# Stick-breaking's v, q and k turned in 32 by 32 blocks on VectorE instead of whole on TensorE

## The chip, the cores and the metric

The kernel runs on one core of one Trainium2 chip. The metric is the device time of one execution in microseconds (us); for a kernel it is the median of its runs. TensorE is the matrix engine, VectorE, ScalarE and GpSimd (POOL in the profile) work on tiles in SBUF and PSUM, and SyncE (SP) issues most of the DMAs. Every engine, and every DMA queue of an engine, works through its instructions in the order in which the program holds them.

## The reference

One layer of a hybrid decoder, batch 1, 1,024 tokens and 16 learned meta tokens in front of them (1,040 positions), width 1,024, all in float32: a half-step SwiGLU, a mixer, another half-step SwiGLU. The mixer projects the normed rows once and splits the columns into an HGRN2 part (4 heads of 128) and a stick-breaking part (8 heads of 64). The change touches stick-breaking alone:

```
q = rms_norm(split_heads(q_raw, 8), q_gain)
k = rms_norm(split_heads(k_raw, 8), k_gain)
v = split_heads(v_raw, 8)
z = q @ k.T / sqrt(64)                      # per head, 128 queries at a time
log_beta = where(allowed, log_sigmoid(z), -inf)
log_keep = where(allowed, log_sigmoid(-z), 0)
suffix = cumsum(log_keep, from the right) - log_keep
out = exp(log_beta + suffix) @ v
```

A key is allowed when it lies strictly before the query. The norm is over the 64 numbers of one head at one position.

## The kernel before

Weights and activations are held as pairs of a rounded part and a remainder (`wh`, `wl` and `xh`, `xl`), and a product is three matmuls: `xh` with `wh`, `xh` with `wl`, `xl` with `wh` (`product`, L242 to L253).

`run` works in stages: the first SwiGLU, the norm, the mixer's projections, the attention woven with the HGRN2 projections, HGRN2, the output projection, the second SwiGLU. The change lies in the projections of stick-breaking. Two heads make one pair, and there are four pairs. `sb_project` (L1260) projects for a pair the 128 columns of k, of v and of q; the columns lie along the partitions and the tokens along the free axis. For pair 0 most of this is done ahead, so only the second half of q is left. The chunks of k and v are 512, 264 and 264 tokens (`CHUNKS`), those of q twice 512 (`HALVES`); a chunk is 24 matmuls. ScalarE copies each chunk from PSUM into `kT`, `vTs` or `qT`.

The weights of a column come by `col_tile` (L237) and `split_w` (L213): SP loads 512 KB into `raw` (two buffers, L225), ScalarE casts `wh` (L232), VectorE makes `wl` (L234); `wh` and `wl` have three buffers each, so a cast waits until the projection three columns earlier is done with its buffer.

The attention wants v with the tokens along the partitions. `sb_v` (L1305) therefore turns `vTs` on TensorE, up to four 128 by 128 tiles in one PSUM bank (`flip`, L1363), splits it into a rounded part and a remainder (ScalarE, VectorE) and stores both with one DMA for each group of four tiles into `vD`. `sb_qk` (L1324) turns q and k in the same way, squares (ScalarE), sums over each head's 64 columns (VectorE), copies the turned tiles to `nat` (VectorE), takes root and reciprocal, multiplies on POOL, turns each tile back on TensorE (`back`, L1355), multiplies by the gain (ScalarE) and splits and stores the result with `put_split` (L1295: ScalarE casts, POOL subtracts, SP stores) into `qD` and `kD`.

`sb_jobs` (L1369) loads q, k and v of one head at a time from these and yields the attention's steps. It begins with stores of zeros into the rows of `vD` that belong to no meta token (L1452).

The order of work: within the stage TensorE's instructions stand as they are written out, in the order in which `weave` (L1585) draws them. It takes a step of the projections, adds the step's cost to a clock, and takes a step of `sb_v` or `sb_qk` whenever that generator's due time has come; each `yield` of these names the cost on TensorE and the delay until the next step. The instructions of the other engines and of SP are put in order by a scheduler with a time model of its own. A pair's generators must have ended before the projections of the second pair after it begin (`join`). After the four pairs the 16 first steps of the HGRN2 projections run (v and f of its head 0), then `braid` mixes attention and the remaining projections.

x at the kernel's beginning is already turned in the manner that the change uses (L983 to L989): VectorE transposes 32 by 32 blocks, and four stores put the blocks in place, in pieces of 128 bytes.

Of the kernel before, what the change touches and what calls it, by code (L numbers as in the profile page):

```python
# [20 lines left out]
P = 128  # L21
D = 1024
KT = D // P
SEQ = 1024
META = 16
T = META + SEQ
# [14 lines left out]
class Block:  # L41
# [1218 lines left out]
    def sb_project(self, p, xh, xl, pool, mix, dst):  # L1260
        nc = self.nc
        vT = pool.tile([P, T], F32, tag="vTs", name="vTs", bufs=2)
        kT = pool.tile([P, T], F32, tag="kT", name="kT", bufs=2)
        qT = pool.tile([P, SEQ], F32, tag="qT", name="qT", bufs=2)
        def use_q(ps, ci, c0, n):
            s = slice(c0 - META, c0 - META + n)
            nc.scalar.copy(qT[:, s], ps)

        def use_k(ps, ci, c0, n):
            nc.scalar.copy(kT[:, c0 : c0 + n], ps)  # L1270

        def use_v(ps, ci, c0, n):
            nc.scalar.copy(vT[:, c0 : c0 + n], ps)

        w = None
        if p == 0:
            w = self.early_w
            for use, x, ci in ((use_k, "k", 0), (use_v, "v", 1), (use_v, "v", 2), (use_v, "v", 0),
                               (use_k, "k", 1), (use_k, "k", 2)):
                use(self.early[x][ci], ci, *CHUNKS[ci])  # L1280
            use_q(self.early["q"][0], 0, *CHUNKS[0])
            self.after_early()
        else:
            yield from self.project(xh, xl, 2560 + P * p, CHUNKS, use_k)
            yield from self.project(xh, xl, 3072 + P * p, CHUNKS, use_v)
        done = [self.sb_v(p, vT, mix, dst[2]), self.sb_qk(p, qT, kT, pool, mix, dst)]
        rest = self.project(xh, xl, 2048 + P * p, HALVES[: 1 if p == 0 else 2], use_q, w)
        if p == 0:
            yield next(rest)
        yield "start", done[0]  # L1290
        yield from rest
        yield "start", done[1]
        return done

    def put_split(self, dst, k, s, t, pool):  # L1295
        nc = self.nc
        n = t.shape[1]
        hi = pool.tile([P, n], F32R, tag="ohi", name="ohi", bufs=2)
        lo = pool.tile([P, n], F32R, tag="olo", name="olo", bufs=2)
        nc.scalar.copy(hi, t)  # L1300
        nc.gpsimd.tensor_sub(lo, t, hi.bitcast(F32))
        nc.sync.dma_start(dst[k, :, 0, s], hi.bitcast(F32))
        nc.sync.dma_start(dst[k, :, 1, s], lo.bitcast(F32))

    def sb_v(self, p, vT, mix, vD):  # L1305

        nc = self.nc
        for j0, nj, m in self.groups:
            ps = self.flip(vT, [self.spots[j0 + j] for j in range(nj)])
            ps = ps.rearrange("p j (h d) -> p j h d", h=2)  # L1310
            t = mix.tile([P, 4, 2, 2, 64], F32R, tag="vhl", name="vhl", bufs=2)
            hi, lo = (t[:m, :nj, :, i, :] for i in range(2))
            nc.scalar.copy(hi, ps[:m])
            nc.vector.tensor_sub(lo, ps[:m], hi.bitcast(F32))
            nc.sync.dma_start(
                vD[p, :m, j0 : j0 + nj, :],
                t.bitcast(F32)[:m, :nj].rearrange("p j h i d -> p j (h i d)"),
            )
            yield 430, 1500

    groups = [(1, 4, P), (5, 4, P), (0, 1, META)]
    spots = [(0, META)] + [(META + P * j, P) for j in range(8)]

    def sb_qk(self, p, qT, kT, pool, mix, dst):  # L1324
        nc = self.nc
        groups, spots = self.groups, self.spots
        ss = pool.tile([P, 17, 2], F32, tag="sbs", name="sbs", bufs=2)
        nc.vector.memset(ss, 1.0)
        nat = pool.tile([P, 17, P], F32, tag="nat", name="nat", bufs=2)
        rows = [(qT, 8 + j0, nj, m, [((j0 - 1 + j) * P, P) for j in range(nj)])  # L1330
                for j0, nj, m in groups[:2]]
        rows += [(kT, j0, nj, m, [spots[j0 + j] for j in range(nj)]) for j0, nj, m in groups]

        for src, j0, nj, m, at in rows:
            ps = self.flip(src, at)
            sq = pool.tile([P, 4, P], F32, tag="sq4", name="sq4", bufs=2)
            nc.scalar.activation(sq[:m, :nj], ps[:m], AF.Square)
            nc.vector.tensor_reduce(
                ss[:m, j0 : j0 + nj, :].rearrange("p j h -> p (j h)"),
                sq[:m, :nj].rearrange("p j (h d) -> p (j h) d", h=2),  # L1340
                mybir.AxisListType.X, ALU.add,
            )
            nc.vector.tensor_copy(nat[:m, j0 : j0 + nj, :], ps[:m])
            yield 430, 600
        nc.scalar.activation(ss, ss, AF.Sqrt, bias=self.eps, scale=1.0 / 64)
        nc.vector.reciprocal(ss, ss)
        for _, j0, nj, m, _ in rows:
            t = nat[:m, j0 : j0 + nj, :].rearrange("p j (h d) -> p j h d", h=2)
            r = ss[:m, j0 : j0 + nj, :].unsqueeze(3).broadcast_to([m, nj, 2, 64])
            nc.gpsimd.tensor_mul(t, t, r)  # L1350
        yield 0, 6000
        for src, j0, nj, m, at in rows:
            ps = self.ptr.tile([P, 4, P], F32, tag="tr", name="back")
            for j in range(nj):
                nc.tensor.transpose(ps[:, j, :m], nat[:m, j0 + j, :], self.ident[:m, :m])  # L1355
            s0, n = at[0][0], (nj - 1) * P + m
            t = mix.tile([P, 512], F32, tag="gt", name="gained", bufs=2)[:, :n]
            gain, to = (self.qg8, dst[0]) if src is qT else (self.kg, dst[1])
            nc.scalar.mul(t, ps.rearrange("p j t -> p (j t)")[:, :n], gain[:, 0:1])
            self.put_split(to, p, slice(s0, s0 + n), t, mix)  # L1360
            yield 430, 1500

    def flip(self, src, spans):  # L1363
        ps = self.ptr.tile([P, len(spans), P], F32, tag="tr", name="flip")
# [4 lines left out]
    def sb_jobs(self, keys, fetch, pool):  # L1369


        nc = self.nc
        qD, kD, vD, oD = keys
# [4 lines left out]
        def load(p, hh):  # L1378
            rows = slice(64 * hh, 64 * hh + 64)
            qs = fetch.tile([P, SEQ], F32R, tag="qs", name="qs", bufs=2)  # L1380
            ks = [fetch.tile([P, T], F32R, tag=f"ks{i}", name="ks", bufs=2) for i in range(2)]
            for i in range(2):
                part = slice(64 * i, 64 * i + 64)
                nc.sync.dma_start(qs.bitcast(F32)[part], qD[p, rows, i])
                for j in range(2):
                    nc.sync.dma_start(ks[j].bitcast(F32)[part], kD[p, rows, j])
            return qs, ks

        def load_v(p, hh):
            v = fetch.tile([P, 9, P], F32R, tag="v", name="v", bufs=2)  # L1390
            nc.sync.dma_start(v.bitcast(F32), vD[p, :, :, hh * P : (hh + 1) * P])
            return v

        def job(p, hh, qs, ks, v, b0):
# [55 lines left out]
            nc.vector.memset(t.bitcast(F32), 0.0)  # L1450
        none = kept["wm"][1][1].rearrange("p b t -> p (b t)").bitcast(F32)[META:]
        for p in range(4):  # L1452
            nc.sync.dma_start(vD[p, META:, 0], none)
        ahead, v = load(*heads[0]), load_v(0, 0)
        yield None
        pool = pools[0]
        for i, (p, hh) in enumerate(heads):
            qs, ks = ahead
            if i:
                v = load_v(p, hh)  # L1460
            for b0 in (0, 6, 2, 4):
# [172 lines left out]
    def run(self):  # L1634
        nc, tc, a = self.nc, self.tc, self.a
# [4 lines left out]
        vD = self.dram.tile([4, P, 9, 2 * P], F32, name="vD")  # L1640
# [6 lines left out]
        n = 512  # L1647
# [8 lines left out]
        with ExitStack() as c0:  # L1656
            with ExitStack() as c1:
# [121 lines left out]
                with tc.manual_schedule(engines={nc.tensor.engine}), ExitStack() as c2:  # L1779
# [46 lines left out]
                    v = [nc.vector] * 2  # L1826
# [202 lines left out]
                with tc.manual_schedule(engines={nc.tensor.engine}):  # L2029
# [20 lines left out]
                    for i, n in enumerate(LEVELS[:5]):  # L2050
                        m = self.masks[:, i, :].rearrange("p (b h r) -> p b h r", h=2, r=n)
# [30 lines left out]
            with tc.manual_schedule(engines={nc.tensor.engine}), ExitStack() as cx:  # L2082
                with ExitStack() as c1:
                    mix = self.pool("mix2", ctx=c1)
# [99 lines left out]
                r = self.inv_rms_rows(sums[1], n, px, ppb)  # L2184
# [55 lines left out]
```

## Time and profile before

| | |
|---|---|
| median of 3 runs | 2021.64 us (2020.22 to 2021.96) |
| the profiled execution | 2020.56 us, its span 2018.8 us |
| granted TensorE clock of that execution | 0.999 |
| stage from the second half of pair 0's q to the first attention step | 748.72 to 899.74 us |
| matmuls that turn q, k, v in it (`flip` and `back`) | 172 |

The profile is one execution of the program. PE is TensorE's matmul, PEld its weight load, DVE VectorE, ACT ScalarE; SPq is SP's DMA queue. Times of instructions count from the span's start. A timeline row has start, duration, engine, line, operation, output and inputs, shapes and count, and behind them, in brackets, the idle time before it and what ended that. Matmuls overlap: their starts are recorded, their ends are modelled, so the distance of two starts is what one costs. A group's row has its count, its busy time in us, the mean of one in ns, and the engine's idle time just before with what ended it.

### The profile page before, as it was taken

How to read it: one execution, taken by the hardware profiler on the slowest of the kernel's cores; microseconds unless marked ns; L12 is line 12 of the kernel's file. 1: busy time of each engine (PE TensorE's matmuls, PEld its weight loads, DVE VectorE, ACT ScalarE, POOL GpSimd, SP SyncE). 2: the span in 40 equal slices, each digit the busy share in tenths (PEclk: the TensorE clock that was granted, in tenths of full speed). 3: DMA queues.
4: the chain of work that ended last, by engine and by line, in shares of the span. 5: the costliest groups of instructions: out<-in, count | busy, mean ns of one | idle time of the engine just before them, and what ended most of it. 6: DMA issues, size and time to landing. Idle time of an engine off the chain costs nothing.

```text
span 2018.8 us, 30806 instructions
## 1 busy us (share of the span) xinstructions
PE 1964.1 (97%) x10940; PEld 1646.2 (82%) x10940; DVE 1356.4 (67%) x2052; ACT 860.8 (43%) x1742; POOL 583.5 (29%) x692
## 2 busy tenths in 40 slices
PE   7999999999999999999999999999999999999998
PEld 6788777777878888888888888777888888888887
DVE  7867667787578663237767667558566766767764
ACT  6423333333444544456666635434132333344443
POOL 3443233332000002334333341320444545530000
PEclk9999999999999999999999999999999999999999
DMA  6266787757985416343545166664533233369363
GB/s 206 83 171 182 227 260 245 241 185 255 327 278 164 131 53 204 123 169 101 139 133 139 55 229 179 167 238 162 194 102 110 101 103 103 106 253 310 116 198 136
DMA packets 315578, 347.19 MB, mean 172 GB/s; under 512 B 61520, under 2 KB 216656, under 8 KB 315424
## 3 DMA queue, kind: packets, MB, share of 16 engines
q1 hardware_dynamic: 297136, 292.18, 46.0%
q0 software_dynamic: 17248, 53.03, 7.5%
q8 instruction: 87, 1.43, 0.3%
q14 instruction: 67, 0.55, 0.1%
q10 hardware_dynamic: 1040, 0.00, 0.0%
HBM read 233.75 MB, written 111.38 MB: 171 GB/s over the span
## 4 chain that ended last, share of the span: by engine, by line
PE 82%; DVE 7%; DMA 5%; issue 3%; ACT 2%; POOL 1%; SPq 0%; DVEq 0%; POOLq 0%; ACTq 0%
PE o L685 18%; PE qb L430 16%; PE qc L430 11%; PE qa L430 10%; PE proj L249 5%; PE proj L251 5%; PE proj L250 5%; PE flip L1366 2%; DMA raw<-in_ffn_w_out_dram 1%; PE wo L250 1%; PE wo L249 1%; PE wo L251 1%; PE mq L937 1%; PE oacc L1436 1%; PE oacc L1438 1%
## 5 line engine op out<-in xcount | busy, mean ns | idle before, releaser
L430 PE MATMUL qb<-T,wh 128*128 128x512 f32 x1056 | 346.0, 391 | 10.1 <-DVE u L462 7.5
L430 PEld LDWEIGHTS qb<-T,wh 128*128 128x128 f32 x1056 | 198.1, 188 | 58.4 <-ACT both L174 5.7
L430 PE MATMUL qa<-B,wh 128*128 128x512 f32 x696 | 227.0, 390 | 2.2 <-DVE sum L513 1.9
L362 DVE TENSOR_TENSOR wl<-s,wh 128x512 fp32r<-128x512 f32 x160 | 183.4, 1147 | 60.4 <-ACT wh L360 59.3
L249 PE MATMUL proj<-xh,wh 128*128 128x512 f32 (+2 forms) x640 | 216.5, 338 | 0.8 <-DVE st L1059 0.7
L685 PE MATMUL o<-t,w 128*128 128x512 f32 x924 | 213.1, 391 | 1.3 <-DVE w L618 1.1
L251 PE MATMUL proj<-xl,wh 128*128 128x512 f32 (+2 forms) x640 | 209.7, 328 | 0.8 <-DVE xl L1821 0.8
L250 PE MATMUL proj<-xh,wl 128*128 128x512 f32 (+2 forms) x640 | 209.9, 328 | 0.0
L685 PE MATMUL o<-parts 128*128 128x512 f32 x924 | 209.9, 389 | 0.0
L430 PE MATMUL qb<-T,wl 128*128 128x512 f32 x528 | 206.0, 390 | 1.5 <-DVE wl L362 1.4
L685 PEld LDWEIGHTS o<-t,w 128*128 128x128 f32 x924 | 172.6, 188 | 39.0 <-DVE w L618 1.5
L685 PEld LDWEIGHTS o<-parts 128*128 128x128 f32 x924 | 173.4, 188 | 36.0
L360 ACT CAST wh<-s 128x512 fp32r<-128x512 f32 x160 | 99.4, 622 | 227.1 <-PE qb L430 168.3
L430 PEld LDWEIGHTS qa<-B,wh 128*128 128x128 f32 x696 | 130.5, 188 | 30.3 <-ACT T L309 2.3
L384 POOL TENSOR_TENSOR s<-raw 128x512 f32<-128x512 f32 x80 | 109.8, 1372 | 153.6 <-DMA raw<-in_ffn_w_in_dram 89.3
L430 PE MATMUL qa<-B,wl 128*128 128x512 f32 x348 | 135.5, 389 | 0.0
L360 ACT CAST wh<-raw 128x512 fp32r<-128x512 f32 x120 | 74.5, 621 | 142.6 <-PE qc L430 103.7
L251 PEld LDWEIGHTS proj<-xl,wh 128*128 128x128 f32 x640 | 120.5, 188 | 12.3 <-DVE xl L1821 1.2
L249 PEld LDWEIGHTS proj<-xh,wh 128*128 128x128 f32 x640 | 120.7, 189 | 11.4 <-DVE st L1059 1.2
L250 PEld LDWEIGHTS proj<-xh,wl 128*128 128x128 f32 x640 | 120.6, 188 | 9.1
L1518 POOL TENSOR_TENSOR sig<-sig,keep 128x144 f32<-128x144 f32 (+3 forms) x64 | 81.4, 1273 | 133.7 <-DVE keep L1512 94.1
L430 PE MATMUL qc<-T,wh 128*128 128x512 f32 x352 | 118.6, 398 | 0.0
(392 smaller groups left out, 4023.2 us busy)
## 6 DMA issues: line engine op xcount, KB each, us to landing
raw<-in_ffn_w_in_dram SPq DMA_DIRECT2D x176, 256.0 KB, 3.5
raw<-in_ffn_w_out_dram SPq DMA_DIRECT2D x121, 256.0 KB, 4.4
w2in<-both SPq DMA_DIRECT2D x28, 512.0 KB, 2.9
raw<-in_w_in_dram SPq DMA_DIRECT2D x25, 512.0 KB, 4.1
ks<-kD SPq DMA_DIRECT2D x32, 260.0 KB, 4.8
wout<-both SPq DMA_DIRECT2D x16, 512.0 KB, 3.8
wh<-w2in SPq DMA_DIRECT2D x27, 256.0 KB, 3.2
wl<-w2in SPq DMA_DIRECT2D x27, 256.0 KB, 3.2
```

The costliest lines, as they stand in the source:

```text
L249: nc.tensor.matmul(ps, wh[:, s], xs, start=k == 0, stop=False)
L250: nc.tensor.matmul(ps, wl[:, s], xs, start=False, stop=False)
L251: nc.tensor.matmul(ps, wh[:, s], xl[:, k, c0 : c0 + n], start=False, stop=k == nk - 1)
L360: nc.scalar.copy(hi, src)
L362: nc.vector.tensor_sub(lo, src, hi.bitcast(F32))
L384: taken(op(t, x, y), False)
L430: nc.tensor.matmul(ps, a[:, k, :], b[:, k, :], start=start and k == 0 and i == 0, stop=k == 3 and i == 2, skip_group_check=True,)
L685: nc.tensor.matmul(banks[bank][m], y[:, m * P : (m + 1) * P], z, start=start and at == 0 and e == 0, stop=q == nq - 1 and e == 2, skip_gro ...
L937: nc.tensor.matmul(ps[at : at + 32, :], self.xm[:, 4 * h + k, :], blocks[i, h][:, k, :], start=h == 0 and kk == 0, stop=h == 1 and kk == 1 ...
L1366: self.nc.tensor.transpose(ps[:m, j, :], src[:, s0 : s0 + m], self.ident)
L1436: nc.tensor.matmul(o[:, c], vj, w[0], start=j == 0, stop=False, skip_group_check=True)
L1518: nc.gpsimd.tensor_mul(sig, sig, keep[:, 1 : nk + 1])
```

## The change

All 172 turning matmuls go. VectorE turns instead, with a block transpose of 32 by 32 blocks from SBUF to SBUF: block (a, b) of the tile is turned in its place, so tokens lie along the 32 partitions of a quarter, and a head's 64 columns are spread over two quarters of the partitions.

- q and k: four block transposes a pair into `nat` (L1351 of the changed kernel; the last of k is 544 wide and takes in 16 columns that POOL sets to one, L1264), squares and sums over 32 columns, then four small ScalarE copies that bring the sum of the other 32 columns across quarters (L1357) and an addition. Root, reciprocal and the products on POOL stay. Four block transposes turn the result back (L1371). The gain is multiplied in `put_split`: ScalarE writes the rounded part straight from it (L1305), and VectorE makes the remainder in one operation (L1306), where POOL did.
- v: three block transposes a pair (L1320), a split as before, and then eight stores a group instead of one, each of 32 partitions in pieces of 128 bytes, so that the stores put the blocks in place (L1331). `vD` has another shape, its loads for the attention are four DMAs of 32 partitions, and the zeros are stored with 16 DMAs instead of 4.
- All steps of `sb_v` and `sb_qk` now yield a cost of 0 on TensorE.

```diff
     def sb_project(self, p, xh, xl, pool, mix, dst):
...
-        kT = pool.tile([P, T], F32, tag="kT", name="kT", bufs=2)
+        kT = pool.tile([P, T + META], F32, tag="kT", name="kT", bufs=2)
+        nc.gpsimd.memset(kT[:, T:], 1.0)
...
-    def put_split(self, dst, k, s, t, pool):
+    def put_split(self, dst, k, s, t, pool, gain=None):
...
-        nc.scalar.copy(hi, t)
-        nc.gpsimd.tensor_sub(lo, t, hi.bitcast(F32))
+        if gain is None:
+            nc.scalar.copy(hi, t)
+            nc.gpsimd.tensor_sub(lo, t, hi.bitcast(F32))
+        else:
+            nc.scalar.mul(hi, t, gain[:, 0:1])
+            nc.vector.scalar_tensor_tensor(
+                lo, t, gain[:, 0:1], hi.bitcast(F32), ALU.mult, ALU.subtract
+            )
...
     def sb_v(self, p, vT, mix, vD):
...
-        for j0, nj, m in self.groups:
-            ps = self.flip(vT, [self.spots[j0 + j] for j in range(nj)])
...
-            hi, lo = (t[:m, :nj, :, i, :] for i in range(2))
-            nc.scalar.copy(hi, ps[:m])
-            nc.vector.tensor_sub(lo, ps[:m], hi.bitcast(F32))
-            nc.sync.dma_start(
-                vD[p, :m, j0 : j0 + nj, :],
-                t.bitcast(F32)[:m, :nj].rearrange("p j h i d -> p j (h i d)"),
-            )
-            yield 430, 1500
+        for c0, nb, m in ((META, 16, 32), (META + 512, 16, 32), (0, 1, META)):
+            y = mix.tile([P, nb, 32], F32, tag="vt", name="vt", bufs=2)
+            nc.vector.transpose(
+                y.rearrange("p b d -> p (b d)"), vT[:, c0 : c0 + 32 * nb]
+            )
+            yield 0, 800
+            t = mix.tile([P, nb, 2, 32], F32R, tag="vhl", name="vhl", bufs=2)
+            nc.scalar.copy(t[:, :, 0], y)
+            nc.vector.tensor_sub(t[:, :, 1], y, t[:, :, 0].bitcast(F32))
+            j0 = 0 if c0 == 0 else 4 + (c0 - META) // 32
+            for b in range(4):
+                for i in range(2):
+                    at = P * (b // 2) + 64 * i + 32 * (b % 2)
+                    nc.sync.dma_start(
+                        vD[p, :m, j0 : j0 + nb, at : at + 32],
+                        t.bitcast(F32)[32 * b : 32 * b + m, :, i],
+                    )
+            yield 0, 1500
...
     def sb_qk(self, p, qT, kT, pool, mix, dst):
...
-            ps = self.flip(src, at)
...
-            nc.vector.tensor_copy(nat[:m, j0 : j0 + nj, :], ps[:m])
-            yield 430, 600
+            y = nat[:, b0 : b0 + nb]
+            nc.vector.transpose(y.rearrange("p b d -> p (b d)"), src[:, c0 : c0 + 32 * nb])
+            sq = pool.tile([P, 17, 32], F32, tag="sq4", name="sq4", bufs=2)[:, :nb]
+            nc.scalar.activation(sq, y, AF.Square)
+            nc.vector.tensor_reduce(ss[:, b0 : b0 + nb], sq, mybir.AxisListType.X, ALU.add)
+            yield 0, 1500
+        for b in range(4):
+            nc.scalar.copy(
+                other[32 * b : 32 * b + 32], ss[32 * (b ^ 1) : 32 * (b ^ 1) + 32]
             )
+        nc.vector.tensor_add(ss, ss, other)
         nc.scalar.activation(ss, ss, AF.Sqrt, bias=self.eps, scale=1.0 / 64)
         nc.vector.reciprocal(ss, ss)
...
         yield 0, 6000
-        for src, j0, nj, m, at in rows:
-            ps = self.ptr.tile([P, 4, P], F32, tag="tr", name="back")
-            for j in range(nj):
-                nc.tensor.transpose(ps[:, j, :m], nat[:m, j0 + j, :], self.ident[:m, :m])
...
+            t = mix.tile([P, 17 * 32], F32, tag="gt", name="gained", bufs=2)[:, : 32 * nb]
+            nc.vector.transpose(t, nat[:, b0 : b0 + nb].rearrange("p b d -> p (b d)"))
...
-            nc.scalar.mul(t, ps.rearrange("p j t -> p (j t)")[:, :n], gain[:, 0:1])
-            self.put_split(to, p, slice(s0, s0 + n), t, mix)
-            yield 430, 1500
+            self.put_split(to, p, slice(c0, c0 + n), t[:, :n], mix, gain)
+            yield 0, 1500
...
-            nc.sync.dma_start(v.bitcast(F32), vD[p, :, :, hh * P : (hh + 1) * P])
+            src = vD[p].rearrange("r (j a) c -> r j a c", a=4)
+            for a in range(4):
+                nc.sync.dma_start(
+                    v.bitcast(F32)[32 * a : 32 * a + 32],
+                    src[:, :, a, hh * P : (hh + 1) * P],
+                )
...
-            nc.sync.dma_start(vD[p, META:, 0], none)
+            nc.sync.dma_start(vD[p, META:, 0], none[:META])
+            for a in range(1, 4):
+                nc.sync.dma_start(vD[p, :, a], none[:32])
```

More of the change, by code (lines that the diff above doesn't have):

```diff
@@ L1307, in sb_v @@
         nc = self.nc
-        for j0, nj, m in self.groups:
-            ps = self.flip(vT, [self.spots[j0 + j] for j in range(nj)])
-            ps = ps.rearrange("p j (h d) -> p j h d", h=2)
-            t = mix.tile([P, 4, 2, 2, 64], F32R, tag="vhl", name="vhl", bufs=2)
-            hi, lo = (t[:m, :nj, :, i, :] for i in range(2))
-            nc.scalar.copy(hi, ps[:m])
-            nc.vector.tensor_sub(lo, ps[:m], hi.bitcast(F32))
-            nc.sync.dma_start(
-                vD[p, :m, j0 : j0 + nj, :],
-                t.bitcast(F32)[:m, :nj].rearrange("p j h i d -> p j (h i d)"),
-            )
-            yield 430, 1500
@@ L1321 @@
-    groups = [(1, 4, P), (5, 4, P), (0, 1, META)]
-    spots = [(0, META)] + [(META + P * j, P) for j in range(8)]
+        for c0, nb, m in ((META, 16, 32), (META + 512, 16, 32), (0, 1, META)):
+            y = mix.tile([P, nb, 32], F32, tag="vt", name="vt", bufs=2)
+            nc.vector.transpose(
+                y.rearrange("p b d -> p (b d)"), vT[:, c0 : c0 + 32 * nb]
+            )
+            yield 0, 800
[11 more added lines that the diff above has]
+            yield 0, 1500
@@ L1324, in sb_qk @@
     def sb_qk(self, p, qT, kT, pool, mix, dst):
         nc = self.nc
[L1326 to L1332, printed above, removed]
@@ L1334, in sb_qk @@
-        for src, j0, nj, m, at in rows:
-            ps = self.flip(src, at)
[L1336 to L1341, printed above, removed]
-            )
-            nc.vector.tensor_copy(nat[:m, j0 : j0 + nj, :], ps[:m])
-            yield 430, 600
+        ss, other = (
+            pool.tile([P, 65], F32, tag=x, name=x, bufs=2) for x in ("sbs", "sbo")
+        )
@@ new lines, in sb_qk @@
+        nat = pool.tile([P, 65, 32], F32, tag="nat", name="nat", bufs=2)
+        rows = [(qT, 0, 0, 16), (qT, 512, 16, 16), (kT, 0, 32, 16), (kT, 512, 48, 17)]
+        for src, c0, b0, nb in rows:
+            y = nat[:, b0 : b0 + nb]
[4 more added lines that the diff above has]
+            yield 0, 1500
@@ L1345, in sb_qk @@
+        for b in range(4):
+            nc.scalar.copy(
+                other[32 * b : 32 * b + 32], ss[32 * (b ^ 1) : 32 * (b ^ 1) + 32]
+            )
+        nc.vector.tensor_add(ss, ss, other)
         nc.scalar.activation(ss, ss, AF.Sqrt, bias=self.eps, scale=1.0 / 64)
         nc.vector.reciprocal(ss, ss)
[L1347 to L1350, printed above, removed]
@@ L1351, in sb_qk @@
-        yield 0, 6000
-        for src, j0, nj, m, at in rows:
-            ps = self.ptr.tile([P, 4, P], F32, tag="tr", name="back")
-            for j in range(nj):
-                nc.tensor.transpose(ps[:, j, :m], nat[:m, j0 + j, :], self.ident[:m, :m])
-            s0, n = at[0][0], (nj - 1) * P + m
-            t = mix.tile([P, 512], F32, tag="gt", name="gained", bufs=2)[:, :n]
+        for _, _, b0, nb in rows:
+            y = nat[:, b0 : b0 + nb]
+            nc.gpsimd.tensor_mul(
+                y, y, ss[:, b0 : b0 + nb].unsqueeze(2).broadcast_to([P, nb, 32])
+            )
@@ L1358, in sb_qk @@
+        yield 0, 6000
+        for src, c0, b0, nb in rows:
+            t = mix.tile([P, 17 * 32], F32, tag="gt", name="gained", bufs=2)[:, : 32 * nb]
+            nc.vector.transpose(t, nat[:, b0 : b0 + nb].rearrange("p b d -> p (b d)"))
+            n = min(32 * nb, (SEQ if src is qT else T) - c0)
             gain, to = (self.qg8, dst[0]) if src is qT else (self.kg, dst[1])
-            nc.scalar.mul(t, ps.rearrange("p j t -> p (j t)")[:, :n], gain[:, 0:1])
-            self.put_split(to, p, slice(s0, s0 + n), t, mix)
@@ L1390, in load_v @@
             v = fetch.tile([P, 9, P], F32R, tag="v", name="v", bufs=2)
-            nc.sync.dma_start(v.bitcast(F32), vD[p, :, :, hh * P : (hh + 1) * P])
+            src = vD[p].rearrange("r (j a) c -> r j a c", a=4)
[3 more added lines that the diff above has]
+                    src[:, :, a, hh * P : (hh + 1) * P],
+                )
             return v
@@ L1639, in run @@
         kD = self.dram.tile([4, P, 2, T], F32, name="kD")
-        vD = self.dram.tile([4, P, 9, 2 * P], F32, name="vD")
+        vD = self.dram.tile([4, 32, 36, 2 * P], F32, name="vD")
         oD = self.dram.tile([4, P, 2, SEQ], F32, name="oD")
```

## The prediction

> **What bounds the kernel now.** I read the page first, then the busy times of the stretch in which stick-breaking's q, k and v are projected and turned, then the instructions of that stretch in order of time.
>
> ```profile
> span 2018.8 us, 30806 instructions
> PE 1964.1 (97%) x10940; PEld 1646.2 (82%) x10940; DVE 1356.4 (67%) x2052; ACT 860.8 (43%) x1742; POOL 583.5 (29%) x692
> PE 82%; DVE 7%; DMA 5%; issue 3%; ACT 2%; POOL 1%; SPq 0%; DVEq 0%; POOLq 0%; ACTq 0%
> ```
> ```profile
> 760.00:780.00 20.00, 20.00 (x136) 18.33 (x136) 6.42 (x12) 8.75 (x17) 6.69 (x6) 1.00 0.46 139
> 840.00:860.00 20.00, 20.00 (x145) 18.66 (x143) 4.90 (x8) 7.71 (x16) 7.98 (x7) 1.00 0.24 78
> ```
>
> TensorE sets the end (82% of the chain). Around the change it has no gap: the second view gives, after each stretch and its length, the busy time of PE, PEld, DVE, ACT and POOL, then granted clock, DMA share and GB/s. PE is busy 20.00 of 20.00 us, VectorE a third, ScalarE under half. So a transpose taken off PE shortens this stage, and every wait newly put before a projection lengthens it by its whole length.
>
> **What the removal brings.** Start times show a transpose's price, the modelled ends do not.
>
> ```profile
> 748.72 0.40 PE L249 MATMUL proj<-xh,wh 128*128 128x512 f32 x1
> ...
> 764.17 0.28 PE L251 MATMUL proj<-xl,wh 128*128 128x264 f32 x1
> 764.29 0.60 PE L1366 MATMUL flip<-ident,kT 128*128 128x128 f32 x4
> 764.64 0.37 PE L249 MATMUL proj<-xh,wh 128*128 128x264 f32 x1
> 764.85 0.28 PE L250 MATMUL proj<-xh,wl 128*128 128x264 f32 x1
> 764.97 0.29 PE L251 MATMUL proj<-xl,wh 128*128 128x264 f32 x1
> ...
> 766.66 0.28 PE L249 MATMUL proj<-xh,wh 128*128 128x264 f32 x1
> ...
> 769.10 0.28 PE L251 MATMUL proj<-xl,wh 128*128 128x264 f32 x1
> 769.22 0.39 PE L249 MATMUL proj<-xh,wh 128*128 128x512 f32 x1
> ...
> 774.56 0.39 PE L251 MATMUL proj<-xl,wh 128*128 128x512 f32 x1
> ...
> 899.74 0.34 PE L1502 MATMUL z<-ks,qs 128*128 128x144 f32 x1
> ```
>
> From 766.66 to 769.10 are 20 steps, 0.122 us each at 264 columns; from 769.22 to 774.56 are 23, 0.232 each at 512. Without the group of four the matmul at 764.97 would stand at 764.53: a group costs 0.44 us. A pair of heads has ten groups (v 2, q and k 4, back 4) and three single ones, taken at a quarter: 4.7 us, over four pairs 18.9. As a check: 748.72 to 899.74 are 151.0 us; the projections in it are 312 matmuls at 0.232, 384 at 0.122 and 96 of 256 columns at some 0.118, together 130.5, which leaves 20.5 for transposes and small waits. I take 19.7 (18.9 to 20.5).
>
> **What it adds to the other engines.** Rows with count, busy time and mean ns:
>
> ```profile
> L983 DVE STREAM_TRANSPOSE xts<-xrow x16: 696/701/712, 117.1 to 355.6; 128x512 f32<-128x512 f32 x16
> ```
> ```profile
> L1350 POOL TENSOR_TENSOR nat<-nat,sbs 128x512 f32<-128x512 f32 x16 | 18.2, 1170 | 98.0 <-DVE sbs L1346 98.0
> L234 DVE TENSOR_TENSOR wl<-raw,wh 128x1024 fp32r<-128x1024 f32 x14 | 17.8, 1274 | 48.2 <-ACT wh L232 48.2
> L232 ACT CAST wh<-raw 128x1024 fp32r<-128x1024 f32 x14 | 14.7, 1053 | 0.0
> L1338 DVE TENSOR_REDUCE sbs<-sq 128x8 f32<-128x512 f32 x16 | 11.0, 686 | 24.6 <-ACT sq L1337 24.4
> L1337 ACT ACTIVATE sq<-flip 128x512 f32<-128x512 f32 x16 | 9.6, 602 | 10.8 <-PE flip L1366 10.7
> L1359 ACT ACTIVATE gained<-back,qg 128x512 f32<-128x512 f32 x8 | 5.5, 690 | 0.3
> L1267 ACT COPY qT<-proj 128x512 f32<-128x512 f32 x8 | 4.7, 591 | 18.0 <-PE proj L251 18.0
> L1346 DVE RECIPROCAL sbs<-sbs 128x34 f32<-128x34 f32 x4 | 1.5, 366 | 1.7 <-ACT sbs L1345 1.7
> L1345 ACT ACTIVATE sbs<-sbs,eps 128x34 f32<-128x34 f32 x4 | 1.3, 323 | 1.0 <-DVE sbs L1338 1.0
> ```
>
> The first row is the block transpose itself: x is already turned so, 0.70 us for 128x512. A pair needs ten of that size and a small one, some 7.1 us of VectorE; the four low parts move there from POOL, while copies from PSUM leave it. At a third busy it has room for all of it. ScalarE loses four multiplications of 0.69 and gains four small copies; I take 0.2 us for each. POOL loses five subtractions. As work on these engines the change costs nothing; what counts is where the wait for it stands.
>
> **What is moved: the weights' casts.** Each projection needs its column's weights cast by ScalarE (wh) and completed by VectorE (wl). Before, a cast runs three projections ahead:
>
> ```profile
> 769.70 1.05 ACT L232 CAST wh<-raw 128x1024 fp32r<-128x1024 f32 x1
> 774.99 0.59 ACT L1273 COPY vTs<-proj 128x512 f32<-128x512 f32 x1 [4.24 <-PE proj L251]
> ```
>
> The cast at 769.70 is for pair 2's k, needed near 796. In the built changed program ScalarE's order is another; cut to the places that matter:
>
> ```
> 599 L1268 TensorCopy qT<-proj 128x512          (pair 1)
> 601 L1353 Activation sq4<-nat 128x512
> ...
> 606 L1361 Activation sbs<-sbs,eps 128x65
> 607 L1305 Activation ohi<-gained,qg8 128x512
> 608 L1305 Activation ohi<-gained,qg8 128x512
> 609 L232 TensorCopy wh<-raw 128x1024           (pair 2's k)
> ```
>
> An engine works in its order, so the weights of pair 2's k now stand behind the whole norm of pair 1's q, which starts only when pair 1's last projection ends; and PE's next instruction is pair 2's k. The same stands before pair 3's k. For pair 1's q the cast stands behind the copies of v and four splits. The other columns' casts stand behind PSUM copies of a projection two or three before theirs, and wait for nothing late.
>
> Gap before pair 2's k (and pair 3's), from the end of q's last matmul: result ready 0.3, copy 0.6, block transpose 0.7, square 0.6, two more squares at half a us, the reductions behind them 1.0, four small copies 0.8, sum 0.2, root 0.35, reciprocal 0.45, two POOL products 2.3, transpose 0.7, ohi 0.7, wh 1.05: 10.75 us. VectorE must first do k's two transposes and two low parts, so wl starts 1.15 later, takes 1.25, and PE's first matmul (wh alone) overlaps 0.23: 12.9 us. Bounds: 10.5 with POOL at 1.0 and no queue on VectorE; 15.5 with POOL at 2.0 and small copies at 0.6. Gap before pair 1's q: ready 0.3, last copy 0.4, two transposes 1.3, then on ScalarE the rest of one cast, another, two ohi and wh (2.95), wl 1.3 less 0.23: 6.0 (4 to 8). Together 31.8 us.
>
> The weights themselves come through SP's queue, where 24 stores of a pair's v now stand, and four or more split stores, ahead of the next load. The same store of 128-byte pieces exists for x:
>
> ```profile
> 126.00 1.97 SPq L986 DMA_DIRECT2D xD<-xts  x4
> ```
> ```profile
> DMA packets 1586, 0.20 MB, mean 99 GB/s; under 512 B 1586, under 2 KB 1586, under 8 KB 1586
> q1 hardware_dynamic: 1586, 0.20, 57.0%
> ```
> ```profile
> DMA packets 25268, 25.60 MB, mean 158 GB/s; under 512 B 2176, under 2 KB 19392, under 8 KB 25255
> q1 hardware_dynamic: 25255, 25.42, 49.4%
> ...
> raw<-in_w_in_dram SPq DMA_DIRECT2D x13, 512.0 KB, 4.1
> ```
>
> An issue takes 0.49 us, so 16 large stores of a pair hold SP for 8 us. The second view is 2 us around 127: 57% of 16 engines is 18.2 us for 1,586 packets, 11.5 ns each. A pair's 8,320 pieces are thus 6 us of all engines. Weights for pair 2's k issue some 13 us after pair 1's v, land 4.1 us later (last row), 6 us into a gap that lasts 12.9 for other reasons: hidden. Without that cover each us would be paid.
>
> The third view is the whole stage: 49.4% of 16 times 162 us for 25,255 packets is 50.7 ns for about 1,006 bytes, so short pieces move bytes at a little over half the rate. The Trainium skill (DMA: Bandwidth & Descriptors, Specifications) asks for at least 512 B per piece and says that a shorter one is read, modified and written; it speaks against these stores, and the rows agree in direction. If each piece cost a long one's 50.7 ns, the third rival below would hold.
>
> **The restart.** No run shows TensorE stopped for 6 or 13 us within work. The nearest rows are the program's start, after 11 us without PE work, and the longest wait later:
>
> ```profile
> 11.01 4.73 PE L736 MATMUL xps<-ident,row 128*128 128x128 f32 x24 [11.01 <-POOL sd L129]
> 15.98 0.50 PE L430 MATMUL qa<-B,wh 128*128 128x512 f32 x1 [0.23 <-ACT B L786]
> 16.32 0.40 PE L430 MATMUL qa<-B,wl 128*128 128x512 f32 x1
> ...
> 19.20 1.18 PE L736 MATMUL xps<-ident,row 128*128 128x128 f32 x8
> ```
> ```profile
> PE qb L430 <- DVE u L462: 7.5, 5, 2.0
> ```
>
> At first a transpose takes 4.73/24, 0.197 us, later 1.18/8, 0.148, and the matmuls from 15.98 step by 0.34: 1.2 us visibly lost, 3 if all of the first 6 us ran at half rate. I take 2.0 for each of three gaps (0 to 3): 6.0.
>
> The Trainium skill (TensorE: Matmul & The Clock Gate, Part 1) says that about 3.4 us without work halve TensorE's clock until about 3.4 us of work have passed. By that estimate each gap costs 1.7 more, 5.1 in all, and the sum ends 0.9 lower; the later waits, 2.0 at most in the last row, would be too short to show it.
>
> **The sum.** 2020.6 (the profiled run) − 19.7 + 31.8 + 6.0 = 2038.7. The profiled run lies 1.1 under the median of the runs shown, inside their spread; I add a small part of that and say 2039.
>
> **Rivals.**
>
> No wait that matters, faster. If PE finds its weights in time it keeps the 19.7: 2001. VectorE's and ScalarE's idle share speaks for it; against it, the order above, in which the cast reads behind products of the very q that PE has just ended. It decides once the three gaps with their restarts fall under 19.7 us together, a norm of some 6 us instead of 10.75.
>
> Gaps and gain balance. If gaps are 3, 8 and 8 and restarts cost nothing: 2020. For it: the restart is unproven. Against: 8 us leave too little even for the ten serial steps at their rows' durations.
>
> The stores flood the queues. At 50.7 ns a piece, 8,192 pieces take 26 us on 16 engines; the load of pair 2's k behind them would land some 32 us after v's end, 21 after q's end, and with its casts (2.3) the two long gaps become 23 each: 2039 + 20 = 2059. For it: the long packets' price; against it: 11.5 ns in the view of x.
>
> **How the numbers follow.** Late casts as computed 0.78, own range 2025 to 2050 (gain 20.5, gaps 25, no slow restart; gain 18.9, gaps 39, restart 9); flooded queues 0.10; balance 0.05; faster 0.07. Eight in ten with parts of the side cases: 2026 to 2055. About 0.2% can be told from no change. Faster takes its rival and a little of the balance, 0.09; same 0.04; slower 0.87.
>
> **What would show it.** After: no flip of qT, kT or vTs on PE; three gaps before projections at 6, 13 and 13 us, ended by wl or wh; 512-column matmuls spaced over 0.3 us after each; the first z at 910 to 917 instead of 899.74; x's price for the new stores. I am wrong if PE has no gap above 3 us there, or if gaps are ended by the weights' DMA.

## The result, and the profile after

| | before | after |
|---|---|---|
| median | 2021.80 us (4 runs, 2020.22 to 2022.20) | 2047.87 us (4 runs, 2043.87 to 2050.03) |
| profiled execution | 2020.6 us | 2050.03 us |
| its span | 2018.8 us | 2048.3 us |
| stage, q's second half to the first z | 151.0 us | 170.4 us |

The ratio is 1.0128 (95% interval 1.011 to 1.0146): 1.3% slower. The forecast was 2039 us, from 2026 to 2055. Of the changed kernel's page, these rows answer to the first rows of the forecast:

```profile
span 2048.3 us, 30583 instructions
PE 1959.5 (96%) x10768; PEld 1640.3 (80%) x10768; DVE 1389.4 (68%) x2088; ACT 854.9 (42%) x1730; POOL 560.9 (27%) x672
PE 84%; DVE 7%; DMA 4%; ACT 2%; issue 2%; POOL 1%; SPq 1%; DVEq 0%; ACTq 0%; POOLq 0%
```

TensorE runs 172 instructions fewer (10940 to 10768), its modelled busy time falls by only 4.6 us, and the span grows by 29.5. So TensorE stands idle, and part of its work is slower. The waits of TensorE between 745 and 960 us say what it stood for. Each row gives the us in total, how many times, and the longest:

```profile
PE proj L249 <- ACT wh L232: 27.1, 3, 11.2
PE proj L250 <- DVE wl L234: 5.1, 3, 2.2
PE z L1523 <- ACT sig L1530: 2.5, 4, 1.6
```

Before, the longest wait in the same stretch was 0.5 us:

```profile
PE z L1502 <- ACT sig L1509: 1.1, 4, 0.5
```

Each of three gaps waits for a cast of weights (`wh`) and then for its low part (`wl`), 32.2 us together. ScalarE's instructions in order of time show what stood ahead of the cast in the second gap:

```profile
801.19 0.58 ACT L1268 COPY qT<-proj 128x512 f32<-128x512 f32 x1 [3.57 <-PE proj L251]
801.67 0.22 ACT L1325 CAST vhl<-vt 128x32 fp32r<-128x32 f32 x1
802.55 1.15 ACT L1353 ACTIVATE sq<-nat 128x512 f32<-128x512 f32 x2 [0.66 <-DVE nat L1351]
803.93 0.66 ACT L1353 ACTIVATE sq<-nat 128x544 f32<-128x544 f32 x1 [0.23 <-DVE sbs L1354]
805.37 1.01 ACT L1357 COPY sbo<-sbs 32x65 f32<-32x65 f32 x4 [0.79 <-DVE sbs L1354]
806.68 0.35 ACT L1361 ACTIVATE sbs<-sbs,eps 128x65 f32<-128x65 f32 x1 [0.30 <-DVE sbs L1360]
809.60 0.72 ACT L1305 ACTIVATE ohi<-gained,qg 128x512 fp32r<-128x512 f32 x1 [2.57 <-DVE gained L1371]
810.61 0.72 ACT L1305 ACTIVATE ohi<-gained,qg 128x512 fp32r<-128x512 f32 x1 [0.28 <-DVE gained L1371]
811.23 1.98 ACT L232 CAST wh<-raw 128x1024 fp32r<-128x1024 f32 x2
```

In brackets stand the engine's idle time and what ended it. The cast waits for nothing of its own: it starts when ohi ends. The whole norm of pair 1's q stands ahead of it, between 801.19 and 811.23. TensorE in the same gap (rows left out at the dots):

```profile
812.31 0.80 PE L249 MATMUL proj<-xh,wh 128*128 128x512 f32 x1 [11.17 <-ACT wh L232]
815.30 0.79 PE L250 MATMUL proj<-xh,wl 128*128 128x512 f32 x1 [2.19 <-DVE wl L234]
815.89 0.63 PE L251 MATMUL proj<-xl,wh 128*128 128x512 f32 x1
...
818.45 0.61 PE L251 MATMUL proj<-xl,wh 128*128 128x512 f32 x1
818.87 0.41 PE L249 MATMUL proj<-xh,wh 128*128 128x512 f32 x1
```

After the gap a 512-column matmul starts every 0.427 us (815.89 to 818.45 in six steps) instead of every 0.232. That is little more than half the pace, for some 3.5 us; the granted clock reads 0.50 there.

A fourth wait stands at the head of the next stage, where before had 0.23 us. First ScalarE, then TensorE:

```profile
928.31 1.04 ACT L232 CAST wh<-raw 128x1024 fp32r<-128x1024 f32 x1 [2.81 <-DMA raw<-in_w_in_dram]
929.26 0.39 ACT L1529 ACTIVATE keep<-z 128x272 f32<-128x272 f32 x1
```
```profile
929.99 0.48 PE L1523 MATMUL z<-ks,qs 128*128 128x456 f32 x1 [1.61 <-ACT sig L1530]
```

A cast waits 2.81 us for its load and holds up the sigmoids behind it, and TensorE stands for 1.61 us. That load was issued at 924.14. The last of v's stores ended on SP at 911.79, with other stores in between, so this row alone doesn't show that v's stores made it late.

### The profile page after: what moved, and what is told of

It is laid out like the page before. It is cut to its first block, busy times and chain, and to the rows that moved or that the text cites. A ratio compares the mean times of both kernels' runs of the same rounds, so it can differ in the third digit from the quotient of the medians.

```text
span 2048.3 us, 30583 instructions
## 1 busy us (share of the span) xinstructions
PE 1959.5 (96%) x10768; PEld 1640.3 (80%) x10768; DVE 1389.4 (68%) x2088; ACT 854.9 (42%) x1730; POOL 560.9 (27%) x672
## 4 chain that ended last, share of the span: by engine, by line
PE 84%; DVE 7%; DMA 4%; ACT 2%; issue 2%; POOL 1%; SPq 1%; DVEq 0%; ACTq 0%; POOLq 0%
PE o L685 18%; PE qb L430 17%; PE qc L430 12%; PE qa L430 10%; PE proj L249 5%; PE proj L250 5%; PE proj L251 5%; DMA raw<-in_ffn_w_out_dram 2%; PE flip L1380 2%; PE wo L250 1%; PE wo L249 1%; PE wo L251 1%; PE mq L937 1%; PE lvl L1159 1%; PE oacc L1455 1%
```

## The experiments

Each ran beside the kernel before on the same chip (medians 2023.19 and 2023.53 us in the two series, 17 and 14 runs), so ratios compare better than times. "Built order" means the order in which the built program holds an engine's instructions. Three theories were open. The first, from the forecast, is that the cast's place in ScalarE's order makes the gaps, and that something about v's stores puts it there. Rival A is that the many short pieces hold up the weights' transfer. Rival B is that the norm's chain costs its length wherever the casts stand.

**v's stores on another queue.**

```
-                    nc.sync.dma_start(
+                    nc.gpsimd.dma_start(
                         vD[p, :m, j0 : j0 + nb, at : at + 32],
```

> Only the queue of v's 96 stores is another: POOL's instead of SP's; every instruction and every piece of 128 bytes stays. In the built order of ScalarE all casts of weights then stand again two or three projections ahead. Theory (the stores' place in SP's queue moves the weights' loads back, and with them the casts): the gaps of 4.7, 11.2 and 11.2 us that end with wh are gone, and so is the wait of 1.6 us behind the first scores; what is left is the gain, 2021.8 - 19.7 = 2002 us, ratio 0.990. Rival A (the short pieces themselves hold up the weights, whichever queue issues them): gaps stay, ended by the weights' DMA, 2040 to 2048. Rival B (the norm's chain of 10.75 us is what PE waits for, wherever the casts stand): gaps of 13 us stay, 2048.

Measured: 2007.38 us, ratio 0.9923 (0.991 to 0.9936). Every gap before a projection is gone (the longest wait there is 0.4 us), with all 128-byte pieces and the whole norm in place: rivals A and B fall. By the ratio it is some 4 us short of what was expected: the waits behind the first scores did not go but grew:

```profile
PE z L1523 <- ACT sig L1530: 4.7, 4, 3.4
```

**The weights' loads on another queue**, the stores left on SP's:

```
-            nc.sync.dma_start(raw.rearrange("p (k f) -> p k f", k=view.shape[1]), view)
+            (nc.scalar if self.raw_apart else nc.sync).dma_start(
+                raw.rearrange("p (k f) -> p k f", k=view.shape[1]), view
+            )
...
+                        self.raw_apart = True
                         self.weave(tasks())
+                        self.raw_apart = False
```

> The stores stay on SP's queue as in the changed kernel; the loads of the weights in this stage are issued by ScalarE instead. In the built order the casts stand two or three projections ahead again. Theory: no gap over 1 us before a projection, 2002 us, ratio 0.990, as with the stores moved; a dozen loads cost ScalarE some us that nothing waits for. Rival A (pieces hold up the transfers): the loads land later than 4.2 us after their issue, and gaps are ended by the weights' DMA, 2010 to 2048. Rival C (a load that ScalarE issues stands behind its own waits): a gap of a few us at each pair, 2010 to 2020.

Measured: 2024.07 us, ratio 1.0003 (0.9995 to 1.0012). The gaps before q and k are gone as the theory says, yet the gain is not there. TensorE now stands once for 14.07 us, in the first columns behind pair 3. SP's queue, ScalarE and TensorE at that place:

```profile
880.41 8.10 SPq L1333 DMA_DIRECT2D vD<-vhl  x16
888.55 1.88 SPq L1062 DMA_DIRECT2D hg_v<-st  x4
```
```profile
890.47 1.28 ACT L1052 ACT_TABLE_LOAD   x1 [8.00 <-DMA hg_v<-st]
```
```profile
892.49 0.58 PE L251 MATMUL proj<-xh,wh 128*128 128x256 f32 x1 [14.07 <-ACT st L1053]
```

Sixteen stores of v hold SP for 8.10 us. Behind them stand the stores that free the four st buffers (the tiles into which ScalarE copies these columns' results), and ScalarE needs a free one to empty TensorE's PSUM bank. None of the three expectations foresaw this place. The cause is of the same kind: what stands behind v's stores in SP's queue is late, here st and not the weights.

**q and k alone**: the changed norm of q and k, with sb_v, load_v, the zero stores and vD's shape of before.

```
     def sb_v(self, p, vT, mix, vD):
+        for j0, nj, m in self.groups:
+            ps = self.flip(vT, [self.spots[j0 + j] for j in range(nj)])
...
-            nc.vector.transpose(
-                y.rearrange("p b d -> p (b d)"), vT[:, c0 : c0 + 32 * nb]
-            )
```

> q and k as in the changed kernel; v is turned by TensorE and stored in three pieces of the longer form as before. Theory (v's stores make the late casts): the casts are early in the built order, no gap over 1 us; the gain is that of 8.5 groups of four per pair, 4 x 8.5 x 0.44 = 15.0, so 2007 us, ratio 0.993. Rival B (the norm of q and k on VectorE, with its chain of 10.75 us, makes the gaps): two gaps of 13 us remain, 2021.8 - 15 + 26 + 4 = 2037.

Measured: 2011.84 us, ratio 0.9938 (0.9924 to 0.9952), where 0.993 was expected. There is no gap before q, k or v, but one wait of 1.64 us for ScalarE's st, at 883.60 in the columns behind pair 3, where nothing over 1 us was expected. The norm and its chain are still there and cost nothing while no cast that TensorE needs at once stands behind them.

**v alone**: sb_v and its stores as changed, sb_qk and put_split of before.

```
     def sb_qk(self, p, qT, kT, pool, mix, dst):
+        for src, j0, nj, m, at in rows:
+            ps = self.flip(src, at)
...
-        for src, c0, b0, nb in rows:
-            y = nat[:, b0 : b0 + nb]
-            nc.vector.transpose(y.rearrange("p b d -> p (b d)"), src[:, c0 : c0 + 32 * nb])
```

> v as in the changed kernel; q and k are turned and normed as before. In the built order the casts for pair 2's k and for the first column behind pair 3 stand behind the copy of q's second half, one square and a split of v; all others are early. Theory: a late cast costs the length of what stands ahead of it: 0.3 + 0.6 + 0.6 + 1.05 + 1.25 and some 0.3, about 4 us at each of the two places, with 1.8 each for the slow matmuls behind them; the gain is 4 x 2.25 x 0.44 = 4.0; 2021.8 - 4 + 8 + 3.6 = 2029, ratio 1.004 (2022 to 2034). Rival B (the chain of the norm on VectorE makes the gaps): none here, 2018. Rival A (the pieces hold up the weights): gaps of 11 us and more ended by the weights' DMA, 2040 and up.

Measured: 2049.43 us, ratio 1.0131 (1.0118 to 1.0144). v's part alone costs as much as the whole change; I had expected 2029. The two places were right. The lengths were not: 10.60 and 7.16 us instead of 4, and another 5.13 behind the first scores. SP's queue, then ScalarE, ahead of the first:

```profile
800.20 4.36 SPq L1328 DMA_DIRECT2D vD<-vhl  x8
804.62 0.59 SPq L225 DMA_DIRECT2D raw<-in_w_in_dram  x1
805.30 3.94 SPq L1328 DMA_DIRECT2D vD<-vhl  x8
```
```profile
800.01 0.22 ACT L1322 CAST vhl<-vt 128x32 fp32r<-128x32 f32 x1
808.95 1.04 ACT L232 CAST wh<-raw 128x1024 fp32r<-128x1024 f32 x1 [8.71 <-DMA raw<-in_w_in_dram]
```

Here the load of pair 2's k is issued only at 804.62, when TensorE is already idle, and lands 4.3 us later (4.1 is the median before). ScalarE is free from 800.2 on. So I had counted what stood ahead of the cast on ScalarE and not what stood ahead of its load on SP. Rival A came near the length, but for another reason than it gave: the load is issued late, and once issued it takes little more than its usual time.

**Only the cast's place.** In the whole change, the squares of q and k keep behind the cast that the program text has before them:

```
-            nc.scalar.activation(sq, y, AF.Square)
+            with self.tc.issue_after(self.cast.ins):
+                nc.scalar.activation(sq, y, AF.Square)
...
-            nc.scalar.copy(hi, raw)
+            self.cast = nc.scalar.copy(hi, raw)
```

> The changed kernel with one edge more: the squares of q and k keep behind the last cast of weights that the program text has before them. SP's order around the loads for pair 2's and 3's k, all stores and all work stay; in ScalarE's order the cast for pair 2's k stands right behind the copy of q's second half and one small split, ahead of the norm. Theory (at these two places it is the cast's place in ScalarE's order that makes the gap): the load is issued at 796.9 and lands at about 801, so the cast runs at 802 and the gap is 0.3 + 0.6 + 0.2 + 1.05 + 1.25 - 0.23, about 3.3 us in place of 13.4, at both places; the gap before pair 1's q stays. 2047.9 - 20.4 = 2027.5, to 2023 if the slow matmuls behind the two gaps go as well; ratio 1.001 to 1.003. Rival (SP's queue alone is to blame, and the loads come too late whatever ScalarE does): gaps of 6 to 13 us remain, ended through the load's DMA, 2033 to 2048. Rival (waiting moves on to the norm, whose lateness then stops later projections): new gaps behind pair 2's v or q, no gain.

Measured: 2027.97 us, ratio 1.0028 (1.0018 to 1.0037); expected 2027.5. ScalarE and TensorE in the gap that was 13.4 us:

```profile
798.31 0.58 ACT L1268 COPY qT<-proj 128x512 f32<-128x512 f32 x1 [3.56 <-PE proj L251]
798.79 0.22 ACT L1326 CAST vhl<-vt 128x32 fp32r<-128x32 f32 x1
798.91 1.05 ACT L232 CAST wh<-raw 128x1024 fp32r<-128x1024 f32 x1
```
```profile
800.01 0.51 PE L249 MATMUL proj<-xh,wh 128*128 128x512 f32 x1 [1.74 <-ACT wh L232]
801.27 0.79 PE L250 MATMUL proj<-xh,wl 128*128 128x512 f32 x1 [0.76 <-DVE wl L234]
```

Of it 1.74 + 0.76 us remain. Before pair 3's k 4.43 + 0.47 us remain, because there the cast waits 2.60 us for its load. The gap before pair 1's q (4.68 + 0.71) stays, as expected. So in the whole change most of the two long gaps is the cast's place in ScalarE's order; a late load behind it has a part of 0 to 3 us.

**The changed kernel again, and TensorE kept at work in the long gaps.**

```
         yield from rest
+        if p in (1, 2):
+            ps = self.ptr.tile([P, 512], F32, tag="tr", name="warm")
+            for i in range(48):
+                nc.tensor.matmul(ps, xh[:, i % 8, :P], xh[:, i % 8, META : META + 512],
+                                 start=i == 0, stop=i == 47)
         yield "start", done[1]
```

> The changed kernel once more, beside the three others and the kernel before on the same chip: ratio 1.0128 again (1.011 to 1.0146), with gaps of 4.7, 11.2 and 11.2 us ended by wh. In its first profile the granted clock also falls to 0.66 in single stretches of 5 us at 60, 415 and 565 us, behind waits of 1.5 to 2.0 us in code that the change doesn't touch; if these stretches belong to the change they come again at the same places, if they are chance they come at others or not at all.

> The changed kernel with 48 matmuls of 512 columns more on TensorE behind q of pairs 1 and 2, in the two long gaps; they add 11.1 us of work each whose result nobody reads. The orders of the other engines stay. Theory (the slow matmuls behind a gap come from TensorE's standing idle): the gaps are filled, k starts as late as before, and its 512-column matmuls are 0.232 us apart from the first instead of 0.426: 1.8 + 2.4 less, 2043.7 us, ratio 1.0107. Rival (the slow steps come from weights just arrived or from what other engines do at that moment): 0.426 stays, ratio 1.0128.

The changed kernel again: 2046.78 us, ratio 1.0119 (1.0105 to 1.0133), the gaps 4.68, 11.17 and 11.23. Kept at work: 2045.44 us, ratio 1.0112 (1.0098 to 1.0126). The intervals overlap, so the times decide nothing; the stage is 168.2 us against 170.4, one profile each. TensorE at the two places, with the filling work in place:

```profile
811.07 0.54 PE L250 MATMUL proj<-xh,wl 128*128 128x512 f32 x1 [2.49 <-DVE wl L234]
811.41 0.63 PE L251 MATMUL proj<-xl,wh 128*128 128x512 f32 x1
...
814.39 0.59 PE L249 MATMUL proj<-xh,wh 128*128 128x512 f32 x1
```
```profile
860.87 0.50 PE L250 MATMUL proj<-xh,wl 128*128 128x512 f32 x1 [2.48 <-DVE wl L234]
861.21 0.39 PE L251 MATMUL proj<-xl,wh 128*128 128x512 f32 x1
861.44 0.40 PE L249 MATMUL proj<-xh,wh 128*128 128x512 f32 x1
```

At 861 the slow steps are gone, as expected. At 811 they are there (0.43 us a step from 811.41 to 814.39), behind a wait for wl of the same length. So the weights' arrival alone doesn't cause them: they arrive alike at both places. The filling does not remove the slow steps for certain, since it left a wait of 2.5 us.

**A version that beats both.** In the first experiment TensorE still waited behind the first scores, and two things were new ahead of it. POOL's products stood behind v's stores on POOL, and some of VectorE's low parts of the weights took long. The low parts (x is their number, then the duration in ns: shortest, median, longest), and VectorE and POOL at a long one:

```profile
L234 DVE TENSOR_TENSOR wl<-raw,wh x14: 1182/1218/5299, 753.3 to 887.7; 128x1024 fp32r<-128x1024 f32 x14
```
```profile
804.61 5.30 DVE L234 TENSOR_TENSOR wl<-raw,wh 128x1024 fp32r<-128x1024 f32 x1
804.70 4.12 POOL L1365 TENSOR_TENSOR nat<-nat,sbs 128x512 f32<-128x512 f32 x4
```

So the four products moved to VectorE, beside v's stores on POOL's queue:

```
-            nc.gpsimd.tensor_mul(
+            nc.vector.tensor_mul(
                 y, y, ss[:, b0 : b0 + nb].unsqueeze(2).broadcast_to([P, nb, 32])
```

> v's stores on POOL's queue as in the first experiment, and the products of q and k with the root's reciprocal on VectorE instead of POOL. There, at pair 3, the products stood on POOL behind 24 stores, a wl of VectorE took 3.62 us instead of 1.27 while POOL multiplied, and PE waited 3.41 us behind the first scores. Theory: these go, the wait falls to 1 us or less with the slow matmuls behind it; 2007.4 - 3 to 5 = 2003 us, ratio 0.990. Rival (the wait comes from pair 3's stores by themselves): it stays, and VectorE's four more products per pair make it no better: 2007 or more.

Measured: 2001.65 us, ratio 0.9895 (0.9881 to 0.9908). VectorE's low parts, and the waits of TensorE from 745 to 900 us:

```profile
L234 DVE TENSOR_TENSOR wl<-raw,wh x14: 1181/1186/1227, 753.4 to 885.1; 128x1024 fp32r<-128x1024 f32 x14
```
```profile
PE z L1523 <- ACT sig L1530: 1.1, 4, 0.5
PE proj L249 <- ACT st L1051: 0.6, 1, 0.6
```

The stage takes 130.4 us, 20.6 less than before: about what the forecast gave for the removal alone. The wait of 3.4 us is gone. The move takes away the products' wait behind the stores and the long low parts at once, so which of the two had made that wait is not shown.

## Why the prediction was right, point by point

- **The gain, 19.7 (18.9 to 20.5).** The last experiment, without gaps, gives 20.6 for the stage; some of it may be small waits of before that went too. The price of 0.44 us for a group of four was nearly right: 20.6 us over the equivalent of 43 groups would be 0.48.
- **The gaps, 6.0 + 12.9 + 12.9 = 31.8.** Measured 5.4 + 13.4 + 13.4 = 32.2 (4.68 and 0.71, 11.17 and 2.19, 11.22 and 2.19). Of the terms of the chain, four small copies took 1.01 (0.8 in the forecast), the root 0.35, ohi 0.72. The built order, out of which the forecast was read, was what the chip did, and moving the cast alone took some 19 us away.
- **The stores' effect, hidden.** This was right for the sum: the load of pair 2's k was issued at 796.86, before the gap began. But I saw in the stores only a load that might land late. v's stores on SP are the common cause: with them on another queue the built order has the casts early again, and the gaps go. Where they are left on SP, something is late in one way or another (the cast by its place in the whole change, the load in v alone, st in the second experiment). Why the scheduler put the cast behind the norm when these stores stood on SP was not examined.
- **The restart, 2.0 each, 6.0.** By the start times the slow steps cost 1.5, 1.7 and 2.4 us, and the first matmul of each gap 0.57 more, 7.3 together. As a check, 151.0 − 20.6 + 32.2 + 7.3 = 169.9 of the 170.4 measured. That 2.0 came so near is partly luck: it was read from the program's start, where the granted clock reads 1.00, while it reads 0.50 behind the gaps.
- **What the sum left out.** The forecast was some 9 us below the median. The sum ended with the stage, while a late load stopped TensorE once more in the next one. From the first z to the next projection (939.31 − 924.28 against 911.00 − 899.74) this took 3.8 us, the wait and a slow spell. That v's stores reach so far is likely but not shown: v alone has 5.13 us there and q and k alone 0.24, but the wait also stood in the first experiment, with these stores on POOL's queue. The rest in the profiled run is a drift of 5.2 us ahead of the stage (q's second half at 753.92 against 748.72), in code that the change doesn't touch. One of the stretches, before and after:

```profile
415.00:420.00 5.00, 4.73 (x49) 3.92 (x50) 5.00 (x8) 0.89 (x2) 1.67 (x1) 1.00 0.48 185
```
```profile
415.00:420.00 5.00, 4.36 (x11) 3.30 (x12) 3.92 (x5) 0.14 (x1) 1.71 (x2) 0.66 0.55 215
```

  The column ahead of the last two is the granted clock: 0.66 over 5 us is 3.4 us at half, 1.7 us lost. Three such stretches (at 60, 415 and 565 us) make 5.1 of the 5.2. In the second profile of the changed kernel the one at 60 is missing. One or two of these three places turn up in seven of the eight experiments' profiles, whatever their edit, and none in the profile of before. Other runs of before seem to have them too: in the first series its runs with a mean granted clock of 0.997 took 2024.39 to 2026.12 us, those with 0.999 took 2018.64 to 2023.19. So they are most likely chance and no part of the change.
- **A sign that was missed.** The forecast looked for the first z at 910 to 917 us; it came at 924.28. The sum itself would put it at 899.74 − 19.7 + 31.8 + 6.0 = 917.8. Of what is over, 5.2 is the drift.
- **The rivals.** No wait that matters (2001 us) is met by the last experiment's 2001.65: it would have been right with the stores on another queue and the products on VectorE. Gaps and gain did not balance, with 32.2 us of gaps instead of 19. Flooded queues fell: with the pieces on POOL's queue no projection waited for its weights. The price of x's pieces held for the new stores, too. The DMA queue's row (packets, MB, share of 16 engines) in the changed kernel from 892 to 912 us, nearly all of it pieces of v:

```profile
q1 hardware_dynamic: 8672, 1.06, 32.3%
```

  32.3% of 16 engines' 20 us for 8,672 packets is 11.9 ns each (11.5 in the forecast).

## What to carry to other kernels

Work taken off the busiest engine pays only if it doesn't put what that engine waits for behind something late. Compare the built order of every engine and of each DMA queue, and look for what now stands in front of the next load or cast. Put many small stores on a queue that nothing urgent shares. When a stall goes after such a move, look for the next thing that waited behind it (here st, then the first scores), and add up the path through the load's issue as well as through its cast.

## What the runs showed of the hardware

**Short waits can halve TensorE's clock.** Take TensorE's waits in the first 1260 us of the ten profiles, and call it a hit when a stretch at granted clock 0.50 lies in the next 8 us. Of 48 waits of over 0.9 and under 1.48 us 1 was a hit, of 37 from 1.48 to 2.1 us 17, of 25 longer ones 24. The bounds were not tried on other kernels, and some of the longer waits belong to one gap. The time without matmuls at each program's start (11.01 us before) is left out; behind them the granted clock reads 1.00 in all ten. A single stretch is about 3.4 us long, sometimes double (behind the 1.61 us at 929.99), and begins up to about 2 us after the wait. The two waits of 2.48 and 2.49 us above went different ways. The Trainium skill (TensorE: Matmul & The Clock Gate, Part 1) tells of a free-running window of about 3.4 us; the length and the play of chance agree with it. It has the clock halve after a whole idle window, and there the measurement decides: waits of about half that length were enough in 17 of 37 cases. So one wait of 2 us can cost 3.7: itself, and 3.4 us at half the clock.

**VectorE stood while POOL multiplied, but not always.** In the first experiment wl took 5.30, 5.26 and 3.62 us where POOL's four products (4.1 us together) ran, and in the last one, with the products on VectorE, 1.23 at most. The Trainium skill (GPSIMD Engine Reference, Specifications) says that POOL shares its SBUF interfaces with VectorE and that VectorE instructions with two SBUF inputs contend there; wl has two, and these rows agree. Before, however, wl ran in the midst of POOL's products and lost little:

```profile
846.08 5.40 POOL L1350 TENSOR_TENSOR nat<-nat,sbs 128x512 f32<-128x512 f32 x5 [16.59 <-DVE sbs L1346]
848.72 1.50 DVE L234 TENSOR_TENSOR wl<-raw,wh 128x1024 fp32r<-128x1024 f32 x1 [2.79 <-ACT wh L232]
```

wl took 1.50 us instead of the usual 1.23, and POOL's five products 5.40 instead of the 4.42 that they took where no wl fell on them. So it was mostly POOL that stood there. What decides which of the two stands, no run here shows.
